# Issuing the stores into HBM from GpSimd instead of SyncE in a two-layer hybrid decoder step

## The chip, the cores and the metric

The kernel runs on one core of one Trainium2 chip. The metric is the device time of one execution in microseconds (us): the median of three runs of the kernel before is 1725.89 us (1721.70 to 1726.36). One further execution was taken with the hardware profiler; every row below comes from it.

## The reference: what is computed

The reference is one inference step of a two-layer decoder on 1088 tokens of width 1024: 1024 tokens of a prompt and 8 samples of 8 tokens, with shared weights. Layer 0 mixes tokens by sliding-window attention (16 query heads, 4 key/value heads of 64, window 128, a learned sink in the softmax); layer 1 by retention with 4 heads (keys of 256, values of 512, chunks of 128 tokens, a carried state). Cut to what matters:

```
for i in range(2):
    h = rms_norm(x, pre_norm[i])
    y, new = swa(h, w_in_attn, sinks, w_out_attn) if i == 0 else ret(h, w_in_ret, w_out_ret)
    x = x + rms_norm(y, post_norm[i])
    x = x + sigmoid(x @ w_ple_gate[i]) * (p[i] @ w_ple[i])

swa:  q, k, v, g = split(h @ w_in); q, k = rope(q), rope(k)
      o = sink_softmax(q k^T / 8, banded mask) v;        y = (o * silu(g)) @ w_out
ret:  q, k, v, g = split(h @ w_in); q, k = rope(q), rope(k) / 16
      per chunk: o = (q k^T * decay) v + q S * decay;    S = gamma^128 S + (k * decay)^T v
      y = (groupnorm(o) * silu(g)) @ w_out
```

The outputs are the new x, the last 128 rotated keys and values (`kwp`, `vwp`; for the samples `kws`, `vws`, 120 old rows and 8 new), and the retention states (`srp`, `srs`).

## The kernel before

All of it is float32, and each large product is made of three float32r matmuls: every operand is split into a rounded part `hi` and a remainder `lo` (`split`, L280: ScalarE casts, VectorE subtracts), and `mm_t` (L128) issues hi*hi, hi*lo, lo*hi (L135 to L137). Activations lie transposed in SBUF (128 features of a tile by tokens), in three token chunks `CH` of 384, 384 and 320. Weights come as 512 KB slots: `load_raw` (L97) issues the load, `prep` (L110) splits a slot and issues the next load (L107).

Activations that are needed again do not stay in SBUF: they are stored to scratch tensors in HBM and loaded back when a unit of attention or retention is due. The stores and the loads that read them back are, in the order of the program:

- `attn_v` (L450): `s_v`, a store of 4 x 128 runs of 512 bytes for each of 8 token blocks (L462), and the outputs `vwp` and `vws` (L467, L471). `attn_k` (L413): `s_k`, four stores of 128 runs a chunk (L424), `s_kn` (L427), `kwp`, `kws` (L437, L439). `attn_q` (L482): for each of four heads `kv`, `s_q`, four stores of 128 runs a chunk (L491), and in the last chunk `s_qs` with the queries of the samples (L495). The split queries and keys lie in `qk_hl`, which has two buffers.
- `attn_load` (L524) loads for unit (kv, n) the queries `qst` (L528), the keys `kwin` (L533) or, for the samples, `qsl` (L541) and the caches. VectorE reorders `qsl` into `qsm` (L544). `attn_scores` (L551) makes the scores (L567, L568), GpSimd copies the sink beside them (L562, L587), VectorE adds the mask and takes the maximum (L556), ScalarE the exponentials (L518). `attn_turn` transposes the probabilities on TensorE (L605), `attn_values` multiplies by the values (L626) and stores the gated result `s_og` (L651).
- `ple` (L307) stores `s_ple` (L322); its input `praw` is loaded at L301. `gate` (L791) stores the residual `s_x2` in layer 0 and the final output `yT` in layer 1 by the same line (L808). `norm_cols` and `resid_cols` have GpSimd raise a sum of squares to the power -1/2 (L239).
- Layer 1: `ret_qkv` stores `s_qk1` (L864) and `s_v1` (L871, L875), `ret_g` stores `s_sg1` (L886), `ret_gate` stores `s_og1`, 4 x 128 runs (L916), `ret_mid` stores the prompt's state (L1012), `ret_sample_in` stores `s_kk` and `s_vv`, eight stores a head (L1037, L1038), `ret_sample_step` stores the states of the samples (L1083), `ret_sample_gate` stores the gated result (L1098), `half_out` stores half an output projection `s_ya` (L1172). `groupnorm` (L891) has GpSimd compute a power (L902) for which VectorE waits (L903). `ret_load`, `ret_load_g` and `ret_sample_load` load what was stored.

In the kernel before every one of these transfers, in both directions, is issued by SyncE, whose queue is worked through in order: an issue that waits (for a landing, for an engine that has to write or free the tile) holds up all issues behind it. GpSimd computes only the few small operations named above.

The order of the work is set in two steps. The program interleaves a main stream of projections with a stream of units (`weave`, L32: after each main step of weight w the units advance by w times a rate; `script`, L41, runs extra work at numbered steps). Then the framework orders each engine's instructions by a simulated timeline (`schedule_with_timeline_sim=True`, L1331), so a change of an issuing engine can also move neighbours within a queue.

Of the kernel before, what the change touches and what calls it, by code (L numbers as in the profile page):

```python
# [16 lines left out]
P = 128  # L17
# [36 lines left out]
class Trunk:  # L54
# [252 lines left out]
    def ple(self, layer, pool, acts):  # L307
        nc = self.nc
        for s in range(2):
            w = self.slot()  # L310
            for pr2 in range(2):
                for c, (c0, n) in enumerate(CH):
                    ps = self.pj.tile([P, 2, 512], F32, name="pj")
                    for j in range(2):
                        f = (pr2 * 2 + j) * P
                        self.mm_t(ps[:, j, :n], w, lambda k: slice(k * 512 + f, k * 512 + f + P), acts, c)
                    if pr2 == 1 and c == 2:
                        self.prep()
                    st = pool.tile([P, 2, 384], F32, name="rp_a", bufs=3)[:, :, :n]
                    nc.scalar.mul(st, ps[:, :, :n], 0.5)  # L320
                    ft = s * 4 + pr2 * 2
                    nc.sync.dma_start(self.s_ple[layer][:, ft:ft + 2, c0:c0 + n], st)  # L322
                    yield n / 200


# [87 lines left out]
    def attn_k(self, pool, acts):  # L413
        nc = self.nc

        def evac(c, ps, c0, n):
            self.norm_rows(c)
            r = self.rope(pool, ps, n, c0)
            m = min(n, TP - c0)
            hl = pool.tile([P, 2, 2, 384], F32R, name="qk_hl")  # L420
            self.split(hl[:, 0, :, :m], hl[:, 1, :, :m], r[:, :, :m])
            for ab in range(2):
                for half in range(2):
                    nc.sync.dma_start(self.s_k[:, ab, half * 32:half * 32 + 32, c0:c0 + m], hl[:, ab, half, :m].bitcast(F32))  # L424
            if c == 2:
                for half in range(2):
                    nc.sync.dma_start(self.s_kn[half * 32:(half + 1) * 32, :, :].rearrange("r k t -> k r t"),  # L427
                                      r[:, half, 256:320])
                for lo, rows, dst in ((128, P, "p"), (256, TS, "s")):
                    pt = self.pa.tile([P, 512], F32, name="pa")  # L430
                    for half in range(2):
                        nc.tensor.transpose(pt[:rows, half * P:(half + 1) * P], r[:, half, lo:lo + rows], self.ident)
                    kn = pool.tile([P, 4, 2, 32], F32, name="knat" + dst, bufs=1)
                    nc.scalar.copy(kn[:rows], pt[:rows, 0:256].rearrange("p (h k r) -> p k h r", h=2, k=4))
                    flat = kn[:rows].rearrange("p k h r -> p (k h r)")
                    if dst == "p":
                        nc.sync.dma_start(self.io["kwp"], flat)  # L437
                    else:
                        nc.sync.dma_start(self.io["kws"][:, 120:128, :], flat)  # L439

        yield from self.pair_t(acts, evac)

# [7 lines left out]
    def attn_v(self, pool, kvp, acts):  # L450
        nc = self.nc
        self.vnew = pool.tile([TS, 256], F32, name="vnew", bufs=1)

        def evac(i, ps):
            r = self.rcol[:, i // 3, i % 3:i % 3 + 1]
            if i < 8:
                st = kvp.tile([P, 4, 2, 64], F32R, name="v_hl", bufs=7)
                pv = ps.rearrange("p (k d) -> p k d", k=4)
                nc.scalar.activation(st[:, :, 0, :], pv, AF.Copy, scale=r)
                nc.vector.scalar_tensor_tensor(out=st[:, :, 1, :], in0=pv, scalar=r, in1=st[:, :, 0, :].bitcast(F32),  # L460
                                               op0=ALU.mult, op1=ALU.subtract)
                nc.sync.dma_start(self.s_v[:, :, i].rearrange("k p h d -> p k h d"), st.bitcast(F32))  # L462
                self.done.add(("v", i))
            if i == 7:
                vn = kvp.tile([P, 256], F32, name="v_out", bufs=2)
                nc.scalar.activation(vn, ps, AF.Copy, scale=r)
                nc.sync.dma_start(self.io["vwp"], vn)  # L467
            if i == 8:
                sh = kvp.tile([TS, 256], F32, name="v_out", bufs=2)
                self.sample_rows(self.vnew, ps, sh)  # L470
                nc.sync.dma_start(self.io["vws"][:, 120:128, :], self.vnew)  # L471
                self.done.add(("v", 8))

        def samp():
            if self.samp is None:
                self.samp = self.sample_cols(pool, acts, "qk_hl", 2)
            return self.samp

        self.samp = None
        yield from self.group_n(acts, samp, evac, True)  # L480

    def attn_q(self, pool, acts, kv):  # L482
        nc = self.nc

        def evac_q(c, ps, c0, n):
            r = self.rope(pool, ps, n, c0)
            m = min(n, TP - c0)
            hl = pool.tile([P, 2, 2, 384], F32R, name="qk_hl")
            self.split(hl[:, 0, :, :m], hl[:, 1, :, :m], r[:, :, :m])
            for j in range(4):  # L490
                nc.sync.dma_start(self.s_q[kv, j * 32:(j + 1) * 32, :, c0:c0 + m].rearrange("r h t -> h r t"),  # L491
                                  hl[:, j // 2, j % 2, :m].bitcast(F32))
            if c == 2:
                for half in range(2):
                    nc.sync.dma_start(self.s_qs[kv, half * 32:(half + 1) * 32].rearrange("r h t -> h r t"),  # L495
                                      r[:, half, 256:320])
            self.done.add(("q", kv, c))

        yield from self.pair_t(acts, evac_q)
# [118 lines left out]
    def attn_values(self, pool, kv, n, u):  # L618
# [29 lines left out]
                    nc.scalar.copy(dst[par * 64:(par + 1) * 64, a], view[:, par, a])  # L648
        sg = self.sg[kv, c][:, :, off:off + cnt]
        nc.vector.scalar_tensor_tensor(out=og, in0=og, scalar=0.5, in1=sg, op0=ALU.mult, op1=ALU.mult)  # L650
        nc.sync.dma_start(self.s_og[2 * kv:2 * kv + 2, :, t0:t0 + cnt].rearrange("a p t -> p a t"), og)  # L651
        self.done.add(("og", kv, n))

    def attn_units(self, pool):
# [136 lines left out]
    def gate(self, pool, layer, acts, ys, sqacc, dst):  # L791

        nc = self.nc
        def evac_pair(pr):
            def evac(c, ps, c0, n, f=0):
# [7 lines left out]
                for j in range(w):  # L803
                    y = ys[f + j][:, c0:c0 + n]
                    nc.vector.tensor_tensor(out=y, in0=y, in1=t[:, j, :], op=ALU.add)
                    if sqacc is not None:
                        self.square_into(pool, sqacc, y, c0, n, pr == 0 and j == 0)
                    nc.sync.dma_start(dst[:, f + j, c0:c0 + n], y)  # L808
            return evac

        ev = [evac_pair(pr) for pr in range(4)]
# [47 lines left out]
    def ret_qkv(self, pool, acts, h):  # L859
        nc = self.nc  # L860
        for which in range(2):
            def evac(c, ps, c0, n):
                r = self.rope(pool, ps, n, c0)
                nc.sync.dma_start(self.s_qk1[h, :, which, :, c0:c0 + n], r)  # L864
            yield from self.pair_t(acts, evac)
        for g in range(2):
            def evac_v(i, ps):
                st = pool.tile([P, 256], F32, name="v1", bufs=4)
                if i < 8:
                    nc.scalar.activation(st, ps, AF.Copy, scale=self.rcol[:, i // 3, i % 3:i % 3 + 1])  # L870
                    nc.sync.dma_start(self.s_v1[h, i, :, g * 256:g * 256 + 256], st)  # L871
                else:
                    sh = pool.tile([P, 256], F32, name="v1", bufs=4)
                    self.sample_rows(st[:64], ps, sh[:64])
                    nc.sync.dma_start(self.s_v1[h, 8, 0:64, g * 256:g * 256 + 256], st[:64])  # L875
                if g:
                    self.done.add(("v1", h, i))
            yield from self.group_n(acts, lambda: self.samp, evac_v)
# [1 line left out]
    def ret_g(self, pool, acts, h):  # L880
        nc = self.nc
        for g in range(2):
            def evac_g(c, ps, c0, n):
                s = pool.tile([P, 2, 384], F32, name="rp_a", bufs=3)[:, :, :n]
                self.silu2(pool, s, ps, c0, n)
                nc.sync.dma_start(self.s_sg1[h, :, 2 * g:2 * g + 2, c0:c0 + n], s)  # L886
                if g:
                    self.done.add(("sg1", h, c))
            yield from self.pair_t(acts, evac_g)
# [18 lines left out]
    def ret_gate(self, pool, on, rows, sg, h, t0):  # L908
        nc = self.nc
        pt = self.pa.tile([P, 512], F32, name="pa")  # L910
        for e in range(4):
# [1 line left out]
        og = sg  # L913
        nc.vector.scalar_tensor_tensor(out=og, in0=pt[:, 0:4 * rows].rearrange("p (e t) -> p e t", e=4), scalar=0.5,
                                       in1=sg, op0=ALU.mult, op1=ALU.mult)
        nc.sync.dma_start(self.s_og1[4 * h:4 * h + 4, :, t0:t0 + rows].rearrange("e p t -> p e t"), og)  # L916
        self.done.add(("og1", h, t0 // P))

    def ret_load(self, pool, h, i, n):
# [55 lines left out]
    def ret_mid(self, pool, h, c, u):  # L975
# [33 lines left out]
            if c < NB - 1:  # L1009
                self.split(sh[:, k], sl[:, k], s[:, k])  # L1010
        if c == NB - 1:
            nc.sync.dma_start(self.io["srp"][h].rearrange("(k p) e -> p k e", p=P), s)  # L1012


    def ret_sample_in(self, pool, h, u):
# [18 lines left out]
                nc.scalar.copy(self.qpad[:, k, g, :, 8 * g:8 * g + 8], src[:, g])  # L1034
        kh, kl = self.k_nat(pool, qk, n, self.rdec[:n, 3, h:h + 1])
        for j in range(4):
            nc.sync.dma_start(self.s_kk[h, :, j], (kh if j < 2 else kl).bitcast(F32))  # L1037
            nc.sync.dma_start(self.s_vv[h, :, j], (vl if j % 2 else vh).bitcast(F32))  # L1038

    def ret_sample_load(self, pool, h, i, u):  # L1040

# [16 lines left out]
    def ret_sample_step(self, pool, h, i, u):  # L1058
# [21 lines left out]
        for j in pair:  # L1080
            s0 = u["s0"][j]
            nc.vector.scalar_tensor_tensor(out=s0, in0=s0, scalar=float(gam ** 8), in1=pds[j], op0=ALU.mult, op1=ALU.add)  # L1082
            nc.sync.dma_start(self.io["srs"][4 * g + j, h, k * P:(k + 1) * P, :], s0)  # L1083
        if i == 7:
            u["on"] = self.groupnorm(pool, po, P, h, 4)

    def ret_sample_gate(self, pool, on, h):
# [7 lines left out]
        for g in range(2):  # L1095
            dst = sg[:, :, 32 * g:32 * g + 32].rearrange("p e (j l) -> p e j l", j=4)
            nc.vector.tensor_tensor(out=dst, in0=rows[:, :, :, 8 * g:8 * g + 8], in1=dst, op=ALU.mult)
        nc.sync.dma_start(self.s_og1[4 * h:4 * h + 4, :, TP:T].rearrange("e p t -> p e t"), sg)  # L1098

    def ret_units(self, pool):  # L1100

# [241 lines left out]
```

## Time and profile before

| | |
|---|---|
| median of three runs | 1725.89 us (1721.70 to 1726.36) |
| profiled execution, device time | 1720.34 us |
| its span, first to last instruction | 1718.4 us |
| its mean granted TensorE clock | 0.989 of full speed |
| instructions | 27977 |
| HBM read and written | 173.45 MB and 99.68 MB |

The profiled execution lies 5.55 us below the median; 1.94 us of its time lie around the span. The engines are named PE (TensorE matmuls), PEld (its weight loads), DVE (VectorE), ACT (ScalarE), POOL (GpSimd) and SP (SyncE); SPq is SyncE issuing transfers, and an issue's duration there is the issuing alone, not the transfer. A row of the chain of waits that begins with DMA is the time from an issue to the landing that released the next step. [...]

### The profile page before, as it was taken

The numbers are of one execution on the slowest core, as the hardware profiler recorded it, in microseconds if no ns is written. First come the engines' busy times: TensorE is split into PE (matmuls) and PEld (weight loads), VectorE is DVE, ScalarE is ACT, GpSimd is POOL, SyncE is SP. The second block draws the span as 40 slices with busy tenths as digits, with TensorE's granted clock in tenths as the row PEclk, the third lists the DMA queues.
The fourth block names the chain that finished last, engine by engine and source line by source line (L and its number), as shares of the span: only waits on it lengthen the run. The fifth ranks groups of instructions, "written<-read, shape, count | busy, mean of one in ns | idle before, by whom it ended". The sixth has DMA issues, their size and how long they took to land.

```text
span 1718.4 us, 27977 instructions
## 1 busy us (share of the span) xinstructions
PE 1676.2 (98%) x10600; PEld 1592.4 (93%) x10600; DVE 986.7 (57%) x2184; ACT 611.8 (36%) x1365; POOL 54.2 (3%) x95
## 2 busy tenths in 40 slices
PE   8969999999999999999999999999999999999998
PEld 7959899898999999899989999999989888999998
DVE  7538777777328674235654466445644675553862
ACT  6225554678424350222132322222232342141321
POOL 0000000000000000000000000000000000000100
PEclk9989999999999999999999999999999999999999
DMA  8433554577513444435545655555455675483342
GB/s 290 146 121 107 165 154 139 155 228 237 165 48 116 147 129 131 123 107 174 163 142 182 183 155 169 152 175 182 143 178 158 226 231 165 159 266 98 109 153 86
DMA packets 233837, 272.99 MB, mean 159 GB/s; under 512 B 25992, under 2 KB 194504, under 8 KB 233672
## 3 DMA queue, kind: packets, MB, share of 16 engines
q1 hardware_dynamic: 233704, 271.22, 50.6%
q8 instruction: 83, 1.36, 0.3%
q14 instruction: 50, 0.41, 0.1%
HBM read 173.45 MB, written 99.68 MB: 159 GB/s over the span
## 4 chain that ended last, share of the span: by engine, by line
PE 86%; DMA 7%; DVE 2%; issue 1%; ACT 1%; SPq 1%; ACTq 0%; DVEq 0%
PE pj L135 20%; PE pj L137 20%; PE pj L136 20%; PE pj L194 4%; PE pj L195 3%; PE pj L196 3%; DMA s_q<-qk_hl 2%; DMA s_k<-qk_hl 1%; PE pa L605 1%; PE pa L1079 1%; PE pa L1068 1%; PE pa L912 1%; DMA s_qs<-rp_a 1%; PE pa L1001 1%; PE pa L943 1%
## 5 line engine op out<-in xcount | busy, mean ns | idle before, releaser
L135 PE MATMUL pj<-act,whi 128*128 128x384 f32 (+1 forms) x2160 | 714.5, 331 | 1.1 <-ACT v L870 0.6
L137 PE MATMUL pj<-act,wlo 128*128 128x384 f32 (+1 forms) x2160 | 709.9, 329 | 0.0
L136 PE MATMUL pj<-act,whi 128*128 128x384 f32 (+1 forms) x2160 | 709.5, 329 | 0.0
L135 PEld LDWEIGHTS pj<-act,whi 128*128 128x128 f32 x2160 | 407.6, 189 | 10.9 <-issue 7.2
L136 PEld LDWEIGHTS pj<-act,whi 128*128 128x128 f32 x2160 | 407.8, 189 | 3.2 <-issue 2.0
L137 PEld LDWEIGHTS pj<-act,wlo 128*128 128x128 f32 x2160 | 407.6, 189 | 2.9 <-issue 2.0
L281 ACT CAST whi<-wraw 128x512 fp32r<-128x512 f32 (+1 forms) x226 | 128.0, 614 | 190.2 <-PE pj L136 148.0
L282 DVE TENSOR_TENSOR wlo<-wraw,whi 128x512 fp32r<-128x512 f32 (+1 forms) x226 | 146.5, 681 | 75.2 <-ACT whi L281 74.7
L194 PE MATMUL pj<-whi,act 128*128 128x256 f32 x528 | 149.2, 286 | 1.1 <-ACT v L870 0.6
L195 PE MATMUL pj<-wlo,act 128*128 128x256 f32 x528 | 148.7, 283 | 0.0
L196 PE MATMUL pj<-whi,act 128*128 128x256 f32 x528 | 147.9, 283 | 0.0
L194 PEld LDWEIGHTS pj<-whi,act 128*128 128x128 f32 x528 | 100.2, 191 | 5.5 <-issue 1.6
L195 PEld LDWEIGHTS pj<-wlo,act 128*128 128x128 f32 x528 | 101.0, 191 | 0.8 <-issue 0.2
L196 PEld LDWEIGHTS pj<-whi,act 128*128 128x128 f32 x528 | 100.5, 191 | 0.3 <-issue 0.2
L518 ACT ACTIVATE s_sb<-s_sb,nm 128x257 f32<-128x257 f32 (+2 forms) x136 | 65.6, 486 | 53.6 <-DVE nm L515 53.5
L870 ACT ACTIVATE v<-pj,rcol 128x256 f32<-128x256 f32 x64 | 29.6, 473 | 120.6 <-PE pj L196 83.6
L330 DVE TENSOR_TENSOR rp_a<-pj,cs 128x768 f32<-128x768 f32 (+1 forms) x39 | 35.5, 911 | 58.6 <-PE pj L137 58.4
L340 DVE TENSOR_TENSOR rp_b<-pj,rbc 128x768 f32<-128x768 f32 (+1 forms) x36 | 32.7, 910 | 49.8 <-PE pj L137 49.8
L282 DVE TENSOR_TENSOR ql<-qk,qh 128x256 fp32r<-128x256 f32 x28 | 11.8, 422 | 80.0 <-ACT qh L281 80.0
L958 ACT ACTIVATE kh<-pa,rdec 128x256 fp32r<-128x256 f32 (+1 forms) x36 | 17.0, 472 | 109.4 <-PE pa L955 108.7
L1082 DVE SCALAR_TENSOR_TENSOR s<-s,pa 128x512 f32<-128x512 f32 x64 | 42.3, 683 | 20.8 <-PE pa L1079 20.6
L902 POOL TENSOR_TENSOR br<-bv,mhalf 128x1 f32<-128x1 f32 x36 | 27.9, 779 | 814.2 <-DVE bv L899 814.2
(208 smaller groups left out, 2302.5 us busy)
## 6 DMA issues: line engine op xcount, KB each, us to landing
wraw<-wt SPq DMA_DIRECT2D x110, 512.0 KB
s<-st SPq DMA_DIRECT2D x64, 256.0 KB
srs<-s SPq DMA_DIRECT2D x64, 256.0 KB
act<-s_og SPq DMA_DIRECT2D x48, 192.0 KB
qst<-s_q SPq DMA_DIRECT2D x32, 256.0 KB
qk<-s_qk SPq DMA_DIRECT2D x32, 256.0 KB
s_v<-v SPq DMA_DIRECT2D x64, 128.0 KB
vv<-s_v SPq DMA_DIRECT2D x32, 256.0 KB
```

The costliest lines, as they stand in the source:

```text
L135: mm(ps, hi[:, sl], a[c][:, 0], start=start and i == 0, stop=False)
L136: mm(ps, hi[:, sl], a[c][:, 1], start=False, stop=False)
L137: mm(ps, lo[:, sl], a[c][:, 0], start=False, stop=stop and i == last)
L194: mm(o, hi, w[0][:, sl], start=start, stop=False)
L195: mm(o, hi, w[1][:, sl], start=False, stop=False)
L196: mm(o, lo, w[0][:, sl], start=False, stop=stop)
L281: self.nc.scalar.copy(hi, x)
L282: self.nc.vector.tensor_tensor(out=lo, in0=x, in1=hi.bitcast(F32), op=ALU.subtract)
L330: nc.vector.tensor_tensor(out=ta, in0=ps, in1=self.cs[:, 0:1, c0:c0 + n].broadcast_to([P, 2, n]), op=ALU.mult)
L340: nc.vector.tensor_tensor(out=g, in0=ps, in1=self.rbc[:, :, c0:c0 + n].broadcast_to([P, 2, n]), op=ALU.mult)
L518: nc.scalar.activation(s[:, h, :], s[:, h, :], AF.Exp, bias=nm[:, h, :], scale=0.125, accum_out=den[:, h:h + 1])
L1082: nc.vector.scalar_tensor_tensor(out=s0, in0=s0, scalar=float(gam ** 8), in1=pds[j], op0=ALU.mult, op1=ALU.add)
```

## The change

In every place below `nc.sync.dma_start` becomes `nc.gpsimd.dma_start`. That is each transfer from SBUF into HBM except two kinds: the copies of the 120 old cache rows (L705, HBM to HBM), and the final output `yT` at L808, where the engine now depends on the layer. All loads stay on SyncE. The diff, one line of each hunk and in full where it is more than the name:

```
@@ ple, L322
-                    nc.sync.dma_start(self.s_ple[layer][:, ft:ft + 2, c0:c0 + n], st)
+                    nc.gpsimd.dma_start(self.s_ple[layer][:, ft:ft + 2, c0:c0 + n], st)
@@ attn_k, L424 (and so L427, L437, L439)
-                    nc.sync.dma_start(self.s_k[:, ab, half * 32:half * 32 + 32, c0:c0 + m], hl[:, ab, half, :m].bitcast(F32))
+                    nc.gpsimd.dma_start(self.s_k[:, ab, half * 32:half * 32 + 32, c0:c0 + m], hl[:, ab, half, :m].bitcast(F32))
@@ attn_v, L462 (and so L467, L471)
-                nc.sync.dma_start(self.s_v[:, :, i].rearrange("k p h d -> p k h d"), st.bitcast(F32))
+                nc.gpsimd.dma_start(self.s_v[:, :, i].rearrange("k p h d -> p k h d"), st.bitcast(F32))
@@ attn_q, L491 (and so L495)
-                nc.sync.dma_start(self.s_q[kv, j * 32:(j + 1) * 32, :, c0:c0 + m].rearrange("r h t -> h r t"),
+                nc.gpsimd.dma_start(self.s_q[kv, j * 32:(j + 1) * 32, :, c0:c0 + m].rearrange("r h t -> h r t"),
                                   hl[:, j // 2, j % 2, :m].bitcast(F32))
@@ gate, L808
-                    nc.sync.dma_start(dst[:, f + j, c0:c0 + n], y)
+                    put = nc.sync if sqacc is None else nc.gpsimd
+                    put.dma_start(dst[:, f + j, c0:c0 + n], y)
...
@@ attn_values L651, ret_qkv L864, L871, L875, ret_g L886, ret_gate L916, ret_mid L1012,
   ret_sample_in L1037, L1038, ret_sample_step L1083, ret_sample_gate L1098, half_out L1172
-        nc.sync.dma_start(...)
+        nc.gpsimd.dma_start(...)
```

## Rows read from the trace of the kernel before

**Rows 1.** The page: busy time, share of the span and instructions of each engine
```profile
PE 1676.2 (98%) x10600; PEld 1592.4 (93%) x10600; DVE 986.7 (57%) x2184; ACT 611.8 (36%) x1365; POOL 54.2 (3%) x95
```

**Rows 2.** Waits of PE, whole span: engine, line, awaited, total us, times, longest
```profile
PE pa L605 <- ACT s_sb L575: 13.2, 2, 12.9
...
PE pa L567 <- issue: 3.8, 1, 3.8
PE pa L626 <- DVE mx L556: 3.3, 1, 3.3
PE pa L567 <- DVE og L632: 3.1, 1, 3.1
...
PE pa L987 <- ACT vh L281: 1.8, 1, 1.8
...
PE pa L1079 <- DMA kh<-s_kk: 0.4, 1, 0.4
```

**Rows 3.** Windows behind PE's idle stretches: busy us by engine, PEclk, DMA share
```profile
123.00:129.00 6.00, 5.42 (x19) 5.43 (x20) 3.69 (x18) 3.36 (x11) 0.19 (x1) 0.50 0.01 2
...
199.00:207.00 8.00, 7.99 (x46) 7.00 (x47) 5.98 (x25) 4.31 (x20) 0.20 (x1) 0.79 0.62 186
...
309.00:316.00 7.00, 7.00 (x39) 6.99 (x37) 4.37 (x11) 3.80 (x12) 0.00 (x0) 0.69 0.68 201
```

**Rows 4.** Timeline of SyncE's issues, 33 to 118 us: start, us, line, tiles, count
```profile
33.96 2.75 SPq L462 DMA_DIRECT2D s_v<-v_hl  x3
...
41.86 3.50 SPq L462 DMA_DIRECT2D s_v<-v_hl  x5
...
54.73 3.14 SPq L424 DMA_DIRECT2D s_k<-qk_hl  x4
65.65 2.59 SPq L533 DMA_DIRECT2D kwin<-s_k  x4
68.28 3.13 SPq L424 DMA_DIRECT2D s_k<-qk_hl  x4
...
97.62 1.25 SPq L528 DMA_DIRECT2D qst<-s_q  x2
...
104.43 2.29 SPq L495 DMA_DIRECT2D s_qs<-rp_a  x2
...
114.74 0.51 SPq L541 DMA_DIRECT2D qsl<-s_qs  x1
```

**Rows 5.** Timeline of VectorE, 61 to 121 us; in brackets idle before and releaser
```profile
61.39 0.96 DVE L282 TENSOR_TENSOR qk_hl<-rp_a,qk_hl 128x768 fp32r<-128x768 f32 x1 [0.90 <-ACT qk_hl L281]
...
95.04 0.48 DVE L333 TENSOR_TENSOR rp_a<-rp_a,rp_b 128x320 f32<-128x320 f32 x1
...
120.56 0.49 DVE L544 COPY qsm<-qsl 64x64 f32<-64x64 f32 x4 [17.84 <-DMA qsl<-s_qs]
```

**Rows 6.** Waits of SyncE's queue between 40 and 130 us, columns as in rows 2
```profile
SPq L528 <- DMA s_q<-qk_hl: 8.7, 2, 5.8
...
SPq L533 <- DMA s_k<-qk_hl: 7.7, 1, 7.7
```

**Rows 7.** The chain that ended last, pieces: start us, us, what
```profile
190.97 5.75 DMA qsl<-s_qs
...
299.12 5.85 DMA praw<-pT
...
719.18 3.64 DMA s_v<-v
...
963.35 3.11 DMA s_kk<-kl
```

**Rows 8.** Groups of GpSimd's instructions: shapes, count, busy us, mean ns, idle before
```profile
L902 POOL TENSOR_TENSOR br<-bv,mhalf 128x1 f32<-128x1 f32 x36 | 27.9, 779 | 814.2 <-DVE bv L899 814.2
L239 POOL TENSOR_TENSOR nr<-nv,mhalf 128x3 f32<-128x3 f32 x6 | 8.7, 1446 | 245.0 <-DVE nv L238 245.0
```

**Rows 9.** One window while only `s_q` stores move, columns as in rows 3
```profile
89.00:96.00 7.00, 7.00 (x42) 7.00 (x41) 5.63 (x9) 2.92 (x5) 0.00 (x0) 1.00 0.27 100
```

More of the change, by code (lines that the diff above doesn't have):

```diff
@@ L423, in evac @@
                 for half in range(2):
-                    nc.sync.dma_start(self.s_k[:, ab, half * 32:half * 32 + 32, c0:c0 + m], hl[:, ab, half, :m].bitcast(F32))
+                    nc.gpsimd.dma_start(self.s_k[:, ab, half * 32:half * 32 + 32, c0:c0 + m], hl[:, ab, half, :m].bitcast(F32))
             if c == 2:
                 for half in range(2):
-                    nc.sync.dma_start(self.s_kn[half * 32:(half + 1) * 32, :, :].rearrange("r k t -> k r t"),
+                    nc.gpsimd.dma_start(self.s_kn[half * 32:(half + 1) * 32, :, :].rearrange("r k t -> k r t"),
                                       r[:, half, 256:320])
@@ L436, in evac @@
                     if dst == "p":
-                        nc.sync.dma_start(self.io["kwp"], flat)
+                        nc.gpsimd.dma_start(self.io["kwp"], flat)
                     else:
-                        nc.sync.dma_start(self.io["kws"][:, 120:128, :], flat)
+                        nc.gpsimd.dma_start(self.io["kws"][:, 120:128, :], flat)
         yield from self.pair_t(acts, evac)
@@ L466, in evac @@
                 nc.scalar.activation(vn, ps, AF.Copy, scale=r)
-                nc.sync.dma_start(self.io["vwp"], vn)
+                nc.gpsimd.dma_start(self.io["vwp"], vn)
             if i == 8:
@@ L470, in evac @@
                 self.sample_rows(self.vnew, ps, sh)
-                nc.sync.dma_start(self.io["vws"][:, 120:128, :], self.vnew)
+                nc.gpsimd.dma_start(self.io["vws"][:, 120:128, :], self.vnew)
                 self.done.add(("v", 8))
@@ L494, in evac_q @@
                 for half in range(2):
-                    nc.sync.dma_start(self.s_qs[kv, half * 32:(half + 1) * 32].rearrange("r h t -> h r t"),
+                    nc.gpsimd.dma_start(self.s_qs[kv, half * 32:(half + 1) * 32].rearrange("r h t -> h r t"),
                                       r[:, half, 256:320])
@@ L650, in attn_values @@
         nc.vector.scalar_tensor_tensor(out=og, in0=og, scalar=0.5, in1=sg, op0=ALU.mult, op1=ALU.mult)
-        nc.sync.dma_start(self.s_og[2 * kv:2 * kv + 2, :, t0:t0 + cnt].rearrange("a p t -> p a t"), og)
+        nc.gpsimd.dma_start(self.s_og[2 * kv:2 * kv + 2, :, t0:t0 + cnt].rearrange("a p t -> p a t"), og)
         self.done.add(("og", kv, n))
@@ L863, in evac @@
                 r = self.rope(pool, ps, n, c0)
-                nc.sync.dma_start(self.s_qk1[h, :, which, :, c0:c0 + n], r)
+                nc.gpsimd.dma_start(self.s_qk1[h, :, which, :, c0:c0 + n], r)
             yield from self.pair_t(acts, evac)
@@ L870, in evac_v @@
                     nc.scalar.activation(st, ps, AF.Copy, scale=self.rcol[:, i // 3, i % 3:i % 3 + 1])
-                    nc.sync.dma_start(self.s_v1[h, i, :, g * 256:g * 256 + 256], st)
+                    nc.gpsimd.dma_start(self.s_v1[h, i, :, g * 256:g * 256 + 256], st)
                 else:
@@ L874, in evac_v @@
                     self.sample_rows(st[:64], ps, sh[:64])
-                    nc.sync.dma_start(self.s_v1[h, 8, 0:64, g * 256:g * 256 + 256], st[:64])
+                    nc.gpsimd.dma_start(self.s_v1[h, 8, 0:64, g * 256:g * 256 + 256], st[:64])
                 if g:
@@ L885, in evac_g @@
                 self.silu2(pool, s, ps, c0, n)
-                nc.sync.dma_start(self.s_sg1[h, :, 2 * g:2 * g + 2, c0:c0 + n], s)
+                nc.gpsimd.dma_start(self.s_sg1[h, :, 2 * g:2 * g + 2, c0:c0 + n], s)
                 if g:
@@ L915, in ret_gate @@
                                        in1=sg, op0=ALU.mult, op1=ALU.mult)
-        nc.sync.dma_start(self.s_og1[4 * h:4 * h + 4, :, t0:t0 + rows].rearrange("e p t -> p e t"), og)
+        nc.gpsimd.dma_start(self.s_og1[4 * h:4 * h + 4, :, t0:t0 + rows].rearrange("e p t -> p e t"), og)
         self.done.add(("og1", h, t0 // P))
@@ L1011, in ret_mid @@
         if c == NB - 1:
-            nc.sync.dma_start(self.io["srp"][h].rearrange("(k p) e -> p k e", p=P), s)
+            nc.gpsimd.dma_start(self.io["srp"][h].rearrange("(k p) e -> p k e", p=P), s)
     def ret_sample_in(self, pool, h, u):
@@ L1036, in ret_sample_in @@
         for j in range(4):
-            nc.sync.dma_start(self.s_kk[h, :, j], (kh if j < 2 else kl).bitcast(F32))
-            nc.sync.dma_start(self.s_vv[h, :, j], (vl if j % 2 else vh).bitcast(F32))
+            nc.gpsimd.dma_start(self.s_kk[h, :, j], (kh if j < 2 else kl).bitcast(F32))
+            nc.gpsimd.dma_start(self.s_vv[h, :, j], (vl if j % 2 else vh).bitcast(F32))
     def ret_sample_load(self, pool, h, i, u):
@@ L1082, in ret_sample_step @@
             nc.vector.scalar_tensor_tensor(out=s0, in0=s0, scalar=float(gam ** 8), in1=pds[j], op0=ALU.mult, op1=ALU.add)
-            nc.sync.dma_start(self.io["srs"][4 * g + j, h, k * P:(k + 1) * P, :], s0)
+            nc.gpsimd.dma_start(self.io["srs"][4 * g + j, h, k * P:(k + 1) * P, :], s0)
         if i == 7:
@@ L1097, in ret_sample_gate @@
             nc.vector.tensor_tensor(out=dst, in0=rows[:, :, :, 8 * g:8 * g + 8], in1=dst, op=ALU.mult)
-        nc.sync.dma_start(self.s_og1[4 * h:4 * h + 4, :, TP:T].rearrange("e p t -> p e t"), sg)
+        nc.gpsimd.dma_start(self.s_og1[4 * h:4 * h + 4, :, TP:T].rearrange("e p t -> p e t"), sg)
     def ret_units(self, pool):
@@ L1171, in evac @@
                 nc.scalar.copy(st, ps)
-                nc.sync.dma_start(self.s_ya[:, pr * 2:pr * 2 + 2, c0:c0 + n], st)
+                nc.gpsimd.dma_start(self.s_ya[:, pr * 2:pr * 2 + 2, c0:c0 + n], st)
             yield from self.pair_t(acts, evac)
```

## The prediction

> **What bounds the kernel now.** I read the page first, then PE's waits, and only then the queues. TensorE is busy for 1676.2 of 1718.4 us [rows 1]; the rest, 42.2 us, is all that any change of transfers could win outright. The list of PE's waits splits it [rows 2]: 12.9 us in one stall at L605, 3.8 us before the first scores at L567, then 3.3 (L626), 3.1 (L567) and 1.8 us (L987). The first four lie in the attention of layer 0. [...]
>
> Why does L605 wait? VectorE idles 17.84 us until `qsl` has landed [rows 5]; the maxima, exponentials and transposes stand behind that copy. `qsl` reads back what the `s_qs` stores wrote. Their source was finished at 95.04 + 0.48 = 95.5 us [rows 5], but SyncE issued them at 104.4 [rows 4]: its queue stood at a `qst` load that waited for an earlier `s_q` landing, 8.7 us in two waits, 5.8 the longest [rows 6]. The same happened a stage earlier: the second chunk of keys was split at 61.39 + 0.96 = 62.35 us [rows 5], but its stores went out at 68.28, behind a `kwin` load at 65.65 [rows 4] that waited 7.7 us for the first chunk's landing [rows 6]. Because `qk_hl` has two buffers, a late landing also delays the split two chunks on. A load that waits for a store holds up unrelated stores: this is what the change takes away.
>
> **The change part by part.** By the loops, 438 stores move: 24 `s_ple`, 12 `s_k`, 2 `s_kn`, 4 outputs, 8 `s_v`, 48 `s_q`, 8 `s_qs`, 40 `s_og`, 24 `s_x2`, 24 `s_qk1`, 72 `s_v1`, 24 `s_sg1`, 36 `s_og1`, 4 `srp`, 32 `s_kk`/`s_vv`, 64 `srs`, 12 `s_ya`. They hold about 86,700 contiguous runs, 128 in a usual store, 512 in `s_v` and most `s_og1`.
>
> *What GpSimd pays* the trace doesn't show: no transfer is issued from it. From below, a store costs what SyncE pays: 3.14 / 4 = 0.79 us for 128 runs, gaps included, and 3.50 / 5 = 0.70 for 512 [rows 4]. From above, it is a program on GpSimd as the power of L239 is, 1.45 us, against 0.78 for L902 [rows 8], and in proportion to the runs: 1.45 us for 128 and 5.8 for 512. I take 1.2 us for 128, nearer to the 1.45 because it too is made by GpSimd's own program, and 2.4 for 512, half of proportion, because SyncE pays nothing extra for them. At the upper end the whole is 86,700 / 128 x 1.45 = 982 us of 1718 beside 54 us of its own work [rows 1]: GpSimd is no bound on the mean, only in bursts.
>
> *The first burst.* `s_v` begins at 33.96 and its last five at 41.86 us [rows 4]. At 2.4 us each, eight end near 41.9 + 5 x 2.4 = 53.9, two outputs near 56.3; the first `s_k` were issued at 54.73 [rows 4], so they start 1.6 us later. The second chunk's stores then go out near 62 instead of 68.3, and what hangs on their landing comes about 6 us earlier. `s_qs` is issued within a store or two of its source, near 97 to 100 instead of 104.4; with the 114.74 - 104.43 = 10.3 us that it took to the load of `qsl` [rows 4] the stall at L605 would end 4 to 7 us sooner, and 2 to 5 more if less queues ahead of it. The 3.8 us before L567 goes, since that load waits for `s_q` stores which land before the queries' last chunk is due. I take 11.5 of the 16.7 us and 3.0 of clock (the 2.7 and a little after the first stall): **-14.5**. Bounds: 0 to -19.7.
>
> *The second and third stall.* Before 199 the same `qsl` took 5.75 us from the store's landing to its own [rows 7]; an earlier `s_qs` wins 2 of 3.1 us and 1 of 1.7 clock: **-3** (0 to -4.8). Before 307 a `praw` load at 299.12 landed after 5.85 us [rows 7]; it has no store to wait for, only SyncE's queue: 3 of 3.3 and 2 of 2.2: **-5** (0 to -5.5).
>
> *What gets later.* Where a store was already issued at once, GpSimd's slower issue and its queue add to store-then-load. At the first retention unit `s_v1` took 3.64 us to land [rows 7], before the 1.8 us stall of L987: **+2** (0 to +5.8). For the samples of the second head the last of four `s_kk` took 3.11 us [rows 7] and PE waits for it already, by 0.4 [rows 2]; four issues on GpSimd are 4 x 1.2 = 4.8 us for 3.14 [rows 4], and a store may stand ahead: **+3** (0 to +8). The power of L239 now stands behind `s_x2` stores at three norms, and PE needs it one step later: **+2** (0 to 3 x 1.45 = 4.4). The last `s_og` and `s_og1` before each output projection: **+1** (0 to +5.8). The 36 powers of L902 can be held up by one store each; VectorE is 57% busy [rows 1] and covers that: 0, or up to 1 us each if it doesn't. The final output stays where it was: 0. The sum is -14.5 - 3 - 5 + 8 = **-14.5 us**: 1705.8 for the profiled execution of 1720.34, which lies 5.55 below the median, so 1725.9 - 14.5 = 1711 as a median.
>
> [...] SyncE's queue loses 438 issues and, what counts, the 7.7 and 8.7 us for which waiting loads kept stores back [rows 6]. [...]
>
> **The rivals.** *The wait only changes its name (no change).* Each stall is a store followed by the load that reads it back. If a store takes GpSimd as much longer to issue and land as it was held up before, some 6 us in the first burst, the new costs of 8 eat what is left: 1726, within 5. For it: 2 to 3 us more per landing in a chain of three landings would do. Against: held-up stores show in SyncE's waits at 5.8 and 7.7 us apiece [rows 6].
>
> *GpSimd's queue is the bound (slower).* Take the upper price in the first burst: eight `s_v` at 5.8 and two outputs end at 34 + 49 = 83 us, and `s_qs` is issued behind 26 further stores at 83 + 26 x 1.45 = 121 instead of 104.4: +17 us, nothing won, and +8 from later: 1751. It decides from the point where 34 + 34 x p + 26 x p passes 104.4 us, a price p of 1.17 us for 128 runs if 512 cost four times that, or 1.6 if they cost twice. For it: that point is close to my estimate. Against: 512 runs cost SyncE no more than 128 [rows 4].
>
> *The engines spread (faster still).* While only `s_q` stores move, the DMA engines are busy to 0.27 [rows 9], 4.3 of 16, so four such stores share the same four engines. If stores from GpSimd spread over more, their landings (57.87 to 65.65, 7.8 us for the first four `s_k` [rows 4]) shrink, and the three stalls vanish with their clock: -19.7 - 4.8 - 5.5 + 8 = -22, 1704; without the later costs 1696. [...]
>
> That the change doesn't do what it says I exclude: by the diff all stores but `yT` and the old rows change engine.
>
> **How the numbers follow.** This kernel's measurement tells 0.3%, 5.2 us, from no change. Chances: forecast 0.42, spread 0.12, no change 0.20, GpSimd's queue 0.26. The forecast loses 0.02 to "same", as its bounds reach there: faster 0.52, same 0.22, slower 0.26. The forecast's own range is 1699 to 1722. For 8 in 10, downwards the range takes in the spread, 1694; upwards it takes in no change and the nearer half of the slower case, 1746.
>
> **What would show it.** Right: the wait L605 <- L575 falls from 12.9 to under 6 us, L567's 3.8 is gone, PEclk in the window that follows is above 0.50, SyncE's stores are no longer in its waits, and stores issued from GpSimd take 1.0 to 1.4 us. `s_k` issues sit at 62 us for the second chunk. Wrong: stores of 512 runs at 4 us or more on GpSimd, a first `s_k` after 65 us, DVE L903 waiting for POOL by more than 30 us in sum, or new stalls of PE of over 10 us between 690 and 1500.

## The result and the profile after

The changed kernel takes 1697.78 us (median of 4 runs, 1695.23 to 1702.73) beside 1726.12 us (1721.70 to 1726.82) for the kernel before on the same chip: a ratio of 0.9845, 95% interval 0.9815 to 0.9875, so 28 us or 1.5% faster. On a second chip the same kernel came to 0.9865 (0.9849 to 0.9880), 24 us faster. The forecast was 1711. The profiled execution takes 1695.23 us, 25.1 less than the 1720.34 of before; its span is 1693.5 us.

The page of the kernel after: engines as in [rows 1], then the DMA queues (packets, MB, share of 16 engines).

```profile
PE 1668.0 (98%) x10600; PEld 1583.5 (94%) x10600; DVE 988.7 (58%) x2184; ACT 612.7 (36%) x1365; POOL 340.0 (20%) x533
...
q1 hardware_dynamic: 141152, 177.94, 35.1%
q0 software_dynamic: 37408, 93.40, 15.7%
```

PE idles 1693.5 - 1668.0 = 25.5 us instead of 42.2, and is busy for 8.2 us less with the same 10600 matmuls: 16.7 + 8.2 = 24.9 us, the whole difference of the spans. The 8.2 us are put down to the granted clock (PEclk, as a share of full speed), which was 0.81, 0.99 and 0.97 in the three windows from 86 to 455 us below and is 1.00 there after. GpSimd has 438 instructions more, the stores, and is still busy for only 20%. PE's waits after (behind L808, lines of this kernel are one higher than before):

```profile
...
PE pa L605 <- ACT s_sb L575: 2.9, 2, 2.2
...
PE pj L135 <- ACT rp_a L320: 2.3, 3, 1.7
PE pa L988 <- ACT vh L281: 1.9, 1, 1.9
...
PE pa L567 <- DMA wraw<-wt: 0.7, 1, 0.7
```

Against [rows 2], L605 fell from 12.9 to 2.2, and the stalls of 3.8, 3.3 and 3.1 us are gone or small; the one before the first retention unit stayed (1.8, now 1.9). Windows of the kernel after, columns as in [rows 3] (the same stretch of time holds somewhat different work before and after):

```profile
57.00:64.00 7.00, 7.00 (x49) 7.00 (x48) 5.01 (x7) 1.88 (x3) 3.13 (x6) 1.00 0.55 136
89.00:96.00 7.00, 7.00 (x42) 7.00 (x41) 4.07 (x7) 1.43 (x3) 3.72 (x6) 1.00 0.75 172
123.00:129.00 6.00, 6.00 (x40) 5.79 (x39) 5.96 (x19) 4.09 (x13) 0.94 (x2) 1.00 0.72 183
86.00:130.00 44.00, 41.00 (x261) 39.74 (x261) 27.33 (x88) 19.67 (x55) 8.05 (x14) 1.00 0.53 147
130.00:300.00 170.00, 169.68 (x1115) 161.59 (x1115) 136.73 (x405) 93.62 (x261) 49.67 (x83) 1.00 0.56 152
300.00:455.00 155.00, 148.52 (x954) 140.46 (x953) 97.82 (x300) 101.83 (x266) 34.60 (x58) 1.00 0.62 196
690.00:960.00 270.00, 266.88 (x1741) 249.39 (x1740) 132.46 (x245) 68.95 (x137) 59.27 (x94) 0.99 0.48 156
960.00:1500.00 540.00, 540.00 (x3358) 493.60 (x3357) 307.72 (x601) 156.94 (x319) 126.24 (x193) 1.00 0.55 179
```

The same stretches of the kernel before, without those of [rows 3] and [rows 9]:

```profile
57.00:64.00 7.00, 7.00 (x49) 7.00 (x48) 5.01 (x7) 1.87 (x3) 0.00 (x0) 1.00 0.26 95
...
86.00:130.00 44.00, 27.27 (x145) 26.66 (x144) 14.42 (x44) 9.39 (x26) 0.19 (x1) 0.81 0.38 118
130.00:300.00 170.00, 166.92 (x1089) 159.09 (x1088) 133.16 (x396) 91.92 (x258) 5.08 (x20) 0.99 0.48 142
300.00:455.00 155.00, 148.95 (x951) 140.94 (x950) 108.29 (x340) 105.88 (x275) 4.10 (x17) 0.97 0.63 190
690.00:960.00 270.00, 266.15 (x1793) 250.32 (x1793) 122.03 (x230) 66.71 (x141) 6.38 (x9) 0.99 0.48 150
960.00:1500.00 540.00, 539.39 (x3346) 490.33 (x3345) 306.35 (x600) 150.80 (x305) 21.52 (x27) 1.00 0.56 175
```

Between 86 and 130 us PE issues 261 matmuls instead of 145. Its idle time there falls from 16.7 to 3.0 us, and the clock no longer drops (1.00 for 0.81): 41.00 / 261 = 0.157 us a matmul against 27.27 / 145 = 0.188. The DMA share while stores move doubles or more, 0.26 to 0.55 and, against [rows 9], 0.27 to 0.75. That belonged to a rival, and the experiments come back to it.

The queues of the kernel after, first SyncE's issues, then GpSimd's (columns as in [rows 4, 5]):

```profile
65.84 3.52 SPq L533 DMA_DIRECT2D kwin<-s_k  x4
...
99.55 0.48 SPq L541 DMA_DIRECT2D qsl<-s_qs  x1
```

```profile
55.01 2.79 POOL L424 DMA_DIRECT2D s_k<-qk_hl  x4 [4.46 <-ACT qk_hl L281]
61.66 2.74 POOL L424 DMA_DIRECT2D s_k<-qk_hl  x4 [3.87 <-ACT qk_hl L281]
...
92.28 1.37 POOL L495 DMA_DIRECT2D s_qs<-rp_a  x2 [3.57 <-DVE rp_a L332]
```

The second chunk's `s_k` goes out at 61.66 us (forecast: near 62; before: 68.28 [rows 4]), `s_qs` at 92.28 (forecast: 97 to 100; before: 104.43; 3 of the 12 us are its source, which is itself ready earlier), and `qsl` is loaded at 99.55 instead of 114.74. The loads that wait for a landing wait no less than before: SyncE's waits between 40 and 130 us are 10.8 us for `s_k` and 13.4 for `s_q`, against 7.7 and 8.7 [rows 6]. What changed is that no store stands behind them. But the first four `s_k` land as late as ever: 55.01 + 2.79 = 57.80, and `kwin` follows at 65.84, 8.0 us after (before: 7.8). GpSimd's groups (busy us, mean ns):

```profile
L872 POOL DMA_DIRECT2D s_v<-v x64 | 35.4, 554 | 167.8 <-ACT v L871 167.6 <-issue 0.2
L491 POOL DMA_DIRECT2D s_q<-qk_hl x48 | 33.4, 701 | 31.3 <-ACT qk_hl L281 24.4 <-DVE qk_hl L282 3.6 <-ACT ob L629 2.0
...
L462 POOL DMA_DIRECT2D s_v<-v_hl x8 | 6.2, 782 | 6.9 <-DVE v_hl L460 6.4 <-DVE rsamp L253 0.3 <-issue 0.2
```

A store costs GpSimd 0.55 to 0.78 us, and 512 runs (L462, 0.78) little more than 128 (L491, 0.70); the sign of 1.0 to 1.4 us did not come. None of the signs of being wrong came either; VectorE waits for the powers of L903 (L902 before) by 12.0 us in sum, 10.2 before.

### The profile page after: what moved, and what is told of

Its sections match the earlier page's. It is cut to its first block, busy times and chain, and to the rows that moved or that the text cites. A ratio compares the mean times of both kernels' runs of the same rounds, so it can differ in the third digit from the quotient of the medians.

```text
span 1693.5 us, 28264 instructions
## 1 busy us (share of the span) xinstructions
PE 1668.0 (98%) x10600; PEld 1583.5 (94%) x10600; DVE 988.7 (58%) x2184; ACT 612.7 (36%) x1365; POOL 340.0 (20%) x533
## 3 DMA queue, kind: packets, MB, share of 16 engines
q0 software_dynamic: 37408, 93.40, 15.7%
## 4 chain that ended last, share of the span: by engine, by line
PE 73%; issue 1%; DMA 0%; POOL 0%; ACT 0%; DVE 0%; POOLq 0%; ACTq 0%
PE pj L135 17%; PE pj L137 17%; PE pj L136 17%; PE pj L194 3%; PE pj L195 3%; PE pj L196 3%; PE pa L1080 1%; PE pa L1069 1%; PE pa L913 1%; PE pa L1002 1%; PE pa L1003 1%; PE pa L1004 1%; PE pa L944 1%; PE pa L987 1%; PE pa L986 1%
## 5 line engine op out<-in xcount | busy, mean ns | idle before, releaser
L872 POOL DMA_DIRECT2D s_v<-v x64 | 35.4, 554 | 167.8 <-ACT v L871 167.6
L1083 DVE SCALAR_TENSOR_TENSOR s<-s,pa 128x512 f32<-128x512 f32 x64 | 42.2, 684 | 24.5 <-PE pa L1080 24.0
L342 ACT ACTIVATE rp_a<-rp_b 128x768 f32<-128x768 f32 (+1 forms) x36 | 29.2, 810 | 73.1 <-DVE rp_b L340 73.1
```

What stands on the lines that cost most here:

```text
L872: nc.gpsimd.dma_start(self.s_v1[h, i, :, g * 256:g * 256 + 256], st)
```

## The experiments

Two theories stood at first. **Queue** (Q in the expectations): loads that wait in SyncE's queue hold back stores, and that alone is taken away. **Spread** (S): the stores from GpSimd run on more engines than the 4.3 of 16 of [rows 9]. The last four runs add a cause that neither named, the shape of the stores.

### One part of the change alone

Only the 70 stores of rotated keys and queries are moved:

```
@@ kernel before, L424, L427, L491, L495
-  nc.sync.dma_start(self.s_k[...] / self.s_kn[...] / self.s_q[...] / self.s_qs[...], ...)
+  nc.gpsimd.dma_start(...)
```

> Only the 70 stores of keys and queries in layer 0 (s_k, s_kn, s_q, s_qs) are issued from GpSimd; the other 368 stay on SyncE. Theory Q (the gain is that these stores no longer stand in SyncE's queue behind loads that wait) expects most of the change's 28 us: 1698 to 1708. Theory S (the gain is that a store issued from GpSimd lands on more DMA engines) expects the same here, 1698 to 1708. A theory that all 438 stores share the gain expects about a sixth of it, 1720 to 1726.

Measured: 1700.87 us beside 1722.19, ratio 0.9870 (0.9837 to 0.9904). PE's waits:

```profile
PE pa L987 <- ACT vh L281: 3.8, 1, 3.8
PE pa L567 <- DMA qst<-s_q: 3.3, 1, 3.3
PE pa L605 <- ACT s_sb L575: 2.4, 3, 1.9
```

The large stall is as small as in the change; what is left are single waits of 3 to 4 us, one of them for a load of queries. Then the other 368 alone, with those four lines left on SyncE:

> The complement: the 70 stores of keys and queries stay on SyncE, the other 368 go to GpSimd. Theories Q and S expect little: 1716 to 1728, with the stall at L605 still near 13 us. If the rest of the stores has its own share (the stalls behind other loads in the attention), 1705 to 1715. If their later costs, which the prediction put at 8 us, are real and only hidden by the gain, 1728 to 1736.

Measured: 1722.01, ratio 0.9991 (0.9976 to 1.0005). SyncE's issues in this second run:

```profile
69.92 3.13 SPq L424 DMA_DIRECT2D s_k<-qk_hl  x4
...
107.91 2.49 SPq L495 DMA_DIRECT2D s_qs<-rp_a  x2
```

The second chunk's keys and `s_qs` are as late as in [rows 4]. So 16% of the moved stores carry the gain, and the other 84% neither win nor cost anything that can be measured.

### The queues separated the other way round

All stores stay on SyncE; the loads that attention waits for go to GpSimd:

```
@@ kernel before, attn_load (L528, L533, L538, L541, L547, L549) and vst (L599)
-  nc.sync.dma_start(u["q"].bitcast(F32), self.s_q[kv, :, :, n * P:(n + 1) * P])
+  nc.gpsimd.dma_start(u["q"].bitcast(F32), self.s_q[kv, :, :, n * P:(n + 1) * P])
...
```

> All stores stay on SyncE as before; instead the loads of the attention units (qst, kwin, knT, qsl, the caches, vst) are issued from GpSimd. Theory Q expects that stores and waiting loads are apart just as well: 1698 to 1712. Theory S expects no gain, 1720 to 1730, since stores from SyncE keep to four engines. GpSimd's sink copies now stand behind waiting loads, which can cost up to 10 us in either.

Measured: 1708.42, ratio 0.9917 (0.9886 to 0.9948). SyncE's stores, then GpSimd's loads:

```profile
81.20 12.06 SPq L491 DMA_DIRECT2D s_q<-qk_hl  x8
...
95.71 1.82 SPq L495 DMA_DIRECT2D s_qs<-rp_a  x2
```

```profile
66.71 2.37 POOL L533 DMA_DIRECT2D kwin<-s_k  x4 [11.65 <-DMA s_k<-qk_hl]
...
107.51 0.54 POOL L541 DMA_DIRECT2D qsl<-s_qs  x1 [11.01 <-DMA s_qs<-rp_a]
```

Some 14 us are won with the stores still on SyncE: the order of one queue is a cause of its own. That GpSimd would bring a load faster is not seen: `qst` and `kwin` land there after 4.7 and 5.1 us (medians), from SyncE in the changed kernel after 4.5 and 4.1. But some 10 us of the change's 24 on this chip are missing, and the rows show where they are not won: eight `s_q` stores hold SyncE for 12.06 us, and `qsl` is loaded 107.51 - (95.71 + 1.82) = 10.0 us after the last `s_qs` was issued, against 99.55 - (92.28 + 1.37) = 5.9 in the change.

Only `s_qs` moved, the eight stores behind the largest stall:

> Only the 8 stores s_qs are issued from GpSimd, everything else as before. Theory Q, with the stall at L605 hanging on that store alone: s_qs goes out near 96 us instead of 104, the stalls at L605 (12.9 us) and before the second head's scores (3.1 us) shrink, the one before L567 (3.8 us) stays: 1704 to 1712. If the s_k and s_q stores have to move with it because qk_hl is freed late, 1715 to 1724.

Measured: 1724.32, ratio 1.0010 (0.9998 to 1.0022): nothing is won, and the time lies at the end of the second range. GpSimd issues, then SyncE's:

```profile
96.65 1.58 POOL L495 DMA_DIRECT2D s_qs<-rp_a  x2 [47.06 <-DVE rp_a L332]
```

```profile
106.22 7.38 SPq L491 DMA_DIRECT2D s_q<-qk_hl  x4
113.72 1.60 SPq L541 DMA_DIRECT2D qsl<-s_qs  x1
```

The stores leave 8 us earlier, but their load still stands behind four `s_q` stores that occupy SyncE for 7.38 us, and not for its own store: SyncE's waits between 80 and 130 us have none for `s_qs`. So the queue also works in the other direction: slow stores hold up loads. The large stall stays:

```profile
PE pa L605 <- ACT s_sb L575: 13.5, 3, 11.7
```

With these stores and the loads of the run above both on GpSimd:

> The kernel with the attention units' loads on GpSimd, and s_qs there too; s_k and s_q stay on SyncE. There the load of qsl followed s_qs by 10 us, against 6 in the changed kernel. If that is because s_qs queues behind s_q on the same four engines (theory S, for this store alone), 4 to 8 us less than the run without it: 1700 to 1705. If GpSimd's queue of loads is what keeps that run back, no difference: 1706 to 1711.

```profile
104.69 0.55 POOL L541 DMA_DIRECT2D qsl<-s_qs  x1 [7.18 <-DMA s_qs<-rp_a]
```

Measured: 1704.86, ratio 0.9900 (0.9882 to 0.9918). The wait is 7.18 us for 11.01, but the interval overlaps that of 0.9917, so by the time it settles nothing.

### What a store's price on GpSimd matters

Every store of the change is cut in two by partitions, so that GpSimd issues twice as many:

```
+def put2(eng, dst, src):
+    n, m = dst.shape[0] // 2, src.shape[0] // 2
+    eng.dma_start(dst[:n], src[:m])
+    eng.dma_start(dst[n:], src[m:])
@@ kernel after, each store
-  nc.gpsimd.dma_start(dst, src)
+  put2(nc.gpsimd, dst, src)
```

> The changed kernel with each GpSimd store cut into two of half the partitions: the same bytes and run lengths, but 876 issues, so that GpSimd pays some 1.2 us for each former store, which is the price that the prediction took for 128 runs. If the prediction's later costs come with that price, 5 to 8 us above the changed kernel: 1703 to 1706. If GpSimd has slack for it, within 4 us: 1694 to 1702.

Measured: 1711.57, ratio 0.9928 (0.9901 to 0.9955), some 11 to 14 us slower than the change (at 0.9865 and 0.9845), and above both expected ranges; the page shows GpSimd busy for 562.0 us. Only with the stores of layer 1 and `s_x2` cut so (`s_ple` left whole), and the change unaltered on the same chip:

> The changed kernel with the stores of layer 1 and s_x2 alone cut into halves; layer 0 as in the change. The prediction put 7 of its 8 us of later costs here, at this price of some 1.1 us a store. If that was right, 5 to 8 us above the changed kernel. If the retention has slack for it and the 14 us of the run with all halves were lost in layer 0, within 3 us of the changed kernel.

> The changed kernel itself, beside the others on the same chip, as their measure: 0.9815 to 0.9875 of the kernel before.

Measured: 1698.58 (0.9862, 0.9840 to 0.9883) and 1699.07 (0.9865, 0.9849 to 0.9880), no difference, though GpSimd is busy for 483.4 us in the first.

So in layer 1 a store may cost GpSimd almost twice as much (143.4 us more for 292 more issues, 0.49 each) and nothing is late. The loss of the run with all halves lies with the stores of layer 0 and `s_ple`, but it isn't shown to be the price: there a half of an `s_k` or `s_q` store holds two heads of 32 rows instead of four, so its shape changed too. GpSimd's waits between 70 and 130 us of the run with all halves show stores that waited for a landing (L51 is `put2`):

```profile
POOL s_q L51 <- DMA s_q<-qk_hl: 6.1, 3, 3.6
```

### The stores' shape

Why do four stores hold SyncE for 7 to 9 us and land 8 us late? All 70 decisive stores write four heads of 32 rows: the outermost dimension of the transfer has four entries, an outer dimension of four. Now the scratch layout is changed so that each writes 128 rows, one from each partition. An `s_q` store still fills the same 128 rows of HBM, in another order. The loads that read them back have to come in pieces of 32 partitions. Nothing leaves SyncE:

```
@@ kernel before, L82 (and so s_k, s_kn, s_qs)
-        self.s_q = scratch("s_q", [4, P, 4, TP])
+        self.s_q = scratch("s_q", [4, 4, P, TP])
@@ L491
-  nc.sync.dma_start(self.s_q[kv, j * 32:(j + 1) * 32, :, c0:c0 + m].rearrange("r h t -> h r t"),
+  nc.sync.dma_start(self.s_q[kv, j, :, c0:c0 + m],
@@ L528
-  nc.sync.dma_start(u["q"].bitcast(F32), self.s_q[kv, :, :, n * P:(n + 1) * P])
+  for j in range(4):
+      nc.sync.dma_start(u["q"][j * 32:j * 32 + 32].bitcast(F32),
+                        self.s_q[kv, j, :, n * P:(n + 1) * P].rearrange("(h r) t -> r h t", h=4))
```

> Nothing is moved to GpSimd: all stores stay on SyncE. Instead the scratch layout of s_k, s_kn, s_q and s_qs is changed so that each of these 70 stores writes 128 rows, one of each partition, instead of four heads of 32 rows; the loads that read them back become 32 partitions each (four for qst instead of one, four for kwin instead of two, two for knT and qsl). Open is why these stores, issued from SyncE, keep only 0.26 of the DMA engines busy, land after 7 to 10 us, and take SyncE 7 to 9 us for four issues when they follow one another, and whether the part of the gain that loads on GpSimd did not bring (about 8 us) lies there. Theory spread (a transfer with an outer dimension of four runs on four engines, and the next waits for them): the DMA share from 57 to 64 us rises to over 0.45, the first four s_k land within 5 us, the third chunk's four issues take SyncE under 4 us, L605 falls from 12.9 to under 7, and the time falls by 8 us or more (1700 to 1714) though nothing left SyncE's queue. Theory queue alone (only the order of waits counts): landings stay at 7 to 10 us, L605 stays over 10, the time is 1718 to 1730, or a few us worse for some 150 more load issues on SyncE at 0.5 to 0.8 us each.

Measured: 1693.35 us beside 1724.74, ratio 0.9823 (0.9806 to 0.9841): a gain of 31 us, larger than the range of either theory had it and no smaller than the change's, with all transfers in SyncE's queue. Behind the first four `s_k`, the window of the kernel before, and of this run:

```profile
57.00:59.00 2.00, 2.00 (x15) 2.00 (x14) 1.39 (x2) 0.00 (x0) 0.00 (x0) 1.00 0.25 82
```

```profile
57.00:59.00 2.00, 2.00 (x15) 2.00 (x15) 1.27 (x2) 0.00 (x0) 0.00 (x0) 1.00 0.84 308
...
86.00:130.00 44.00, 44.00 (x287) 43.55 (x286) 30.25 (x96) 21.63 (x60) 0.79 (x3) 1.00 0.48 139
```

The same stores occupy the engines to 0.84 for a short time (from 59 to 61 us it is 0.07) instead of 0.25 for a long one (57 to 65 us), 308 against 82 GB/s. In the window named in the expectation, 57 to 64 us, the share is 0.40 and misses its sign of over 0.45; the other signs came. At the line of L605 the largest wait is 1.7 us, and from 86 to 130 us PE doesn't idle at all: 287 matmuls. SyncE's issues in this run:

```profile
54.85 1.86 SPq L424 DMA_DIRECT2D s_k<-qk_hl  x4
60.39 3.44 SPq L535 DMA_DIRECT2D kwin<-s_k  x7
...
93.19 1.81 SPq L491 DMA_DIRECT2D s_q<-qk_hl  x4
```

Four `s_q` stores take SyncE 1.81 us, and `kwin` can be loaded at 60.39 instead of 65.65 [rows 4]. The same four stores in the kernel before:

```profile
106.81 7.45 SPq L491 DMA_DIRECT2D s_q<-qk_hl  x4
```

The same layout in the changed kernel:

> The changed kernel (stores on GpSimd) with the same scratch layout: stores of 128 rows, loads of 32 partitions. Theory spread: if from GpSimd these stores are spread already, little is left, 1693 to 1701, the landings of s_k and s_q fall from 7 to 8 us to 4 to 6, and the issue on GpSimd stays at 0.7 us; if the layout also shortens the stores' landing the stall of L605 (2.2 to 5.3 us) goes and it beats the change by 2 to 5 us. Theory queue alone: as the change, 1697 to 1701, or slower by 3 to 8 us for the 150 more loads on SyncE.

Measured: **1683.87 us**, ratio 0.9769 (0.9752 to 0.9787), 9.5 us below the layout alone in the same batch and below every range expected. This version beats both kernels. Its largest wait at the line of L605 (here L609):

```profile
PE pa L609 <- ACT s_sb L579: 0.6, 1, 0.6
```

Since the layout also cut the loads, both kernels were run with the loads cut and the stores left as they were:

```
@@ both kernels, L528 (and so L533, L538, L541)
-  nc.sync.dma_start(u["q"].bitcast(F32), self.s_q[kv, :, :, n * P:(n + 1) * P])
+  for j in range(4):
+      nc.sync.dma_start(u["q"][j * 32:j * 32 + 32].bitcast(F32),
+                        self.s_q[kv, j * 32:j * 32 + 32, :, n * P:(n + 1) * P])
```

> Control for the layout on SyncE: the loads of qst, kwin, knT and qsl are cut into pieces of 32 partitions as there, but the scratch layout and the stores stay as in the kernel before (four heads of 32 rows a store, SyncE). If the gain of the layout run (1693.35, 31 us) lay in the stores' outer dimension of four, this run has none of it: L605 stays at 11 to 14 us, four s_q stores in a row still take SyncE over 6 us, the time is 1720 to 1735. If it lay in the loads' smaller pieces, the time falls to 1694 to 1705 with the stores as slow as before.

Measured: 1744.72 beside 1723.12, ratio 1.0122 (1.0102 to 1.0143): slower by 21 us, worse than expected, and with stores as slow as before. SyncE's issues and PE's largest wait:

```profile
92.24 9.04 SPq L529 DMA_DIRECT2D qst<-s_q  x8
...
108.28 8.03 SPq L491 DMA_DIRECT2D s_q<-qk_hl  x4
```

```profile
PE pa L610 <- ACT s_sb L580: 20.5, 4, 15.2
```

> The same control for the changed kernel: stores on GpSimd in the old layout, loads of qst, kwin, knT and qsl in pieces of 32 partitions. If the 14 us by which layout and change beat the change came from the stores, s_q still lands after 7 to 8 us and the time is 1696 to 1703; if from the loads, it is 1683 to 1688.

Measured: 1698.35, ratio 0.9853 (0.9834 to 0.9871), as the change. So the layout's gain isn't the loads' smaller pieces; it is the stores', in whatever of the two they do better, landing or issuing. The landing of the stores (count, KB each, median us from issue to landing) in the change, in this control, and with the layout on top of the change:

```profile
s_q<-qk_hl POOLq DMA_DIRECT2D x32, 192.0 KB, 7.7
...
s_k<-qk_hl POOLq DMA_DIRECT2D x8, 192.0 KB, 7.1
```

```profile
s_q<-qk_hl POOLq DMA_DIRECT2D x32, 192.0 KB, 7.7
```

```profile
s_q<-qk_hl POOLq DMA_DIRECT2D x32, 192.0 KB, 2.7
...
s_k<-qk_hl POOLq DMA_DIRECT2D x8, 192.0 KB, 4.1
```

## Why the prediction was right in sign and place, and short by half

**Right: where the time lay.** The gain stands in the first 130 us and in layer 0's attention. Of the signs that were named these came: `s_k` near 62 us, L605 under 6, L567's 3.8 gone, the clock after the first stall at 1.00.

**The number was less right than the range.** The forecast of 1711 has half of the gain, and 1697.78 lies just below the forecast's own range of 1699 to 1722. It falls into the wide range, 1694 to 1746, only because that was drawn down for the rival of the spread, whose mechanism did not hold as it was put. That part is luck.

**Right: the gains.** The forecast took 11.5 + 2 + 3 = 16.5 us of idling and 3 + 1 + 2 = 6 of clock from the three stalls, 22.5 in all. Its clock terms are estimates from [rows 3], the clock short of 1.00 times PE's busy time: 0.50 x 5.42 = 2.7, 0.21 x 8 = 1.7, 0.31 x 7 = 2.2. Measured over the whole span: 16.7 and 8.2. By stretch, from the windows, PE's idle time went from 16.7 to 3.0 between 86 and 130, from 3.1 to 0.3 between 130 and 300, and stayed (6.0, 6.5) between 300 and 455: there the stall of L626 went, short ones took its place, and what was won is clock (0.97 to 1.00). The `praw` load did leave SyncE's queue earlier, at 284.07 us instead of 299.12 [rows 7]. So the third stall's 3 us of idling were not won; the first gave 13.7 for 11.5.

**Wrong: "what gets later", +8 us.** This term of the sum measured nothing. PE's idle time fell from 3.9 to 3.1 us between 690 and 960 and from 0.6 to 0.0 between 960 and 1500; the 368 other stores moved alone cost nothing (0.9991), and doubling GpSimd's issues in layer 1 costs nothing either. L987's +2 measured 0.1, and the waits for `s_kk` and the norms did not grow. Without this term the sum would have been -22.5, against -25.1 measured. The price was set too high as well, 1.2 and 2.4 us a store for 0.70 and 0.78 measured (that a store costs GpSimd what a program of its own does was an assumption), but that alone didn't make the term wrong: with the stores cut in halves layer 1 paid some 1.1 us a store and nothing was late (2.4 us for 512 runs was not reached). The term charged issues that nothing stood waiting for. The cheap bound, SyncE's own 0.79 and 0.70 [rows 4], was the right one for both shapes. At that price the slower rival was far away: its threshold was 1.17 us.

**Half of the cause.** "A load that waits for a store holds up unrelated stores" is true: with the loads on GpSimd, 14 us are won while the stores still take SyncE as long (12.06 us for eight `s_q`) and land as late (`kwin` follows at 66.71 us, before at 65.65). But the prediction took the landing itself, 7 to 8 us, as given. It need not be: the same stores in 128 rows, from the same queue, win 31 us. The first four `s_k` land within 60.39 - (54.85 + 1.86) = 3.7 us, and the stores no longer stop SyncE; which of the two wins more was not separated. The row that pointed to it was read, the share of 0.27 in [rows 9], 4.3 engines of 16, and was given to a rival with a chance of 0.12.

**The rivals.** "The wait only changes its name" is ruled out by the interval. "The engines spread" came closest in number (1704 or 1696) and its first half is seen, the DMA share of 0.55 and 0.75; but its mechanism, shorter landings, fails where it was put: the first `s_k` land after 8.0 us as before. What GpSimd avoids is the standstill of the issuing queue, 2.74 us for four stores where SyncE needs 7 to 9 when they follow others. Its number came close with the later costs at nothing (1696), a term that its mechanism has no part in.

**The engines kept busy.** In the 2 us from 57 on, SyncE's stores of four heads keep 0.25 of the 16 engines busy and its stores of 128 rows 0.84. Which engines they are no run shows: that four stores share the same four was the author's estimate from the 4.3 of [rows 9]. And the shape isn't all of it: even with the layout mended the move to GpSimd still gives -9.5.

**Open.** Why a store of four heads holds SyncE's issue and not GpSimd's, and why it lands no sooner from GpSimd although more engines are busy, no row names. Of the 10 us between the change and the loads on GpSimd, what belongs to the stores' issue and what to GpSimd's sink copies standing behind waiting loads was not separated. The framework's reordering of neighbours on PE was not tried alone, and in layer 0 the price of the key and query stores was never doubled without changing their shape.

## What to carry to other kernels

When a load waits long for a store that feeds it, look first at the DMA share while only these stores move: where it is a small fraction (0.27 here), look at the store's outer dimension (four here); giving these stores 128 rows won at least as much (31 us) as moving all stores to another queue (24 and 28). Then keep stores and the loads that wait for their landings in different queues (another 9.5 us here), whole groups at a time, since moving one kind alone (`s_qs`, 0 us here) left its load behind the others. SyncE's rows were the better guide to a store's price on GpSimd here (0.79 and 0.70 us for 0.70 and 0.78), and the price cost nothing where nobody waited for the store (1698.58 us with layer 1's in halves, 1699.07 without).

## What had not been expected of the hardware

- How long SyncE takes to issue a store depends on the store's shape and on what stands ahead: four `s_q` stores of four heads take 3.43 us from 85.37 us on in the kernel before and 7.45 from 106.81 on, directly behind `s_qs`, 8.03 with the loads cut; of 128 rows they take 1.81.
- The same store's landing, issued from GpSimd, is 7.7 us with an outer dimension of four and 2.7 with 128 rows, while GpSimd issues one in 0.70 and 0.55 us (`s_q`, mean of 48).
- GpSimd's stores moved 93.40 MB in 37408 packets, 2.5 KB each. SyncE's queue lost 92552 packets and 93.28 MB by them (233704 and 271.22 before), 1.0 KB each.
- Cutting the loads alone, 165 more issues (`qst` 96, `kwin` 64, `qsl` and `knT` 5), cost 21 us on SyncE's crowded queue and nothing that can be measured once the stores had left it.
